# Projections between the blocks of two attentions, in a two-layer streaming encoder on one core

## The chip, the cores and the metric

One Trainium2 chip (trn2), one of its cores. The time is the device time of one execution in microseconds (us). Five engines work side by side, each on its own list of instructions: TensorE (matrix products and transposes, results in PSUM), VectorE, ScalarE, GpSimd, and SyncE, which here only issues DMA transfers. In the profile they are PE (PEld for its loads of the stationary operand), DVE, ACT, POOL and SP; a q behind the name is the part of an engine that issues DMAs.

## The reference

Two groups of tokens, 1024 of a prompt and 32 of a sample, pass through two post-norm layers with the same weights. Cut to what matters here, a layer is

```
(cq, kva, gq, gk, gv, gz, ga, gb, fq, fk, fv, ff) = split_cols(x @ w_in, IN_SPLITS)
o_a = attention(q_a, k_a, v_a, chunk_causal)                # latent: from low-rank cq and kva
o_b, s_new, conv_new = gated_deltanet(gq, gk, gv, gz, ...)  # 4 heads of 128
o_c = attention(fq, fk_all, fv_all, frame_causal, fcum)     # forgetting: fcum, running sum of log forgets
mix = jnp.concatenate([o_a, o_b, o_c], -1) @ w_out
x = layer_norm(ALPHA * x + mix, ...)
x = layer_norm(ALPHA * x + memory_attention(x, mem_k, mem_v, w_xq, w_xo), ...)
x = layer_norm(ALPHA * x + jnp.square(jax.nn.relu(x @ w_ff1)) @ w_ff2, ...)
```

with `mem_k = mem_prompt @ w_mk` and `mem_v = mem_prompt @ w_mv`, which depend on no activation. Both attentions have four heads with values of 64 features and sweep the 1024 queries in eight blocks of 128; block b reads the keys up to its own end, 128 (b + 1) of them. All is float32, and the caches, keys, values and states are outputs too.

## The kernel before, in words

Activations lie feature-major: features on the partitions, the 1024 + 32 tokens along the free axis, cut in three chunks of 352. Each operand of a large product is split in a rounded high part and the rest, and three products (high x high, high x low, low x high) add up in PSUM: `mm3`, lines 99 to 101. A projection's step (`proj`) is one chunk of one tile of 128 output features, 8 x 3 = 24 such products. Its weights come as a unit (`unit`): two DMAs on SP of 256 KB into two staging buffers (`ws`), a rounding on ScalarE (line 94) and a difference on VectorE (95), into two of eight buffers `w`. Other things share these eight: values, cached keys, unsplit weights.

A layer (`layer`) emits its work in this order: projections of delta-rule head 0 and a small tile `misc`; the memory's keys and values (`mem_kv`, 128 records on lines 1254 and 1267); the gates (from `misc`, first instruction line 249); delta-rule heads 0 to 3, each with serial chains and projections of the next head beside them; the sample's part of the delta rule; the low-rank projections (`mla_lora`); the forgetting attention's queries, keys and values (`fox_proj`, 12 steps of queries and keys, 9 of values) woven with keys and values of the cached latent rows (`mla_past`, 6 steps); the latent attention; the forgetting attention; the output projection of the mix, and the rest of the layer. Queries, keys and values of both attentions go to DRAM and are read back (`mla_head`, `fox_head`, `load_v`), one buffer `u` (six of 17 KB a partition) for a head.

Order: SP's DMA list is in the order written. On the other engines a planner at build time orders the instructions: of those that its model holds ready it takes the one emitted first. So what is emitted later fills gaps, if its operands and buffers are there.

Attention (`attend`, 744; pairs of heads `hp`, blocks `b`): for both heads the scores of a block are put in PSUM, in one piece up to 512 keys and in two beyond (banks `"wwwto"`: three of w, one of t, two of o), their maxima taken (758), a scale formed (760, 761), and the exponentials taken with their sums (767). The product with the values (`attend_out`, 786) of a block is put off until after the first exponentials of the next one (`later`): ScalarE copies the weights that TensorE turned by tiles of 128 keys (797, 799), TensorE multiplies them with the values (802), and the result goes to the mix in DRAM by POOL's queue. PSUM has eight banks: w 3, s 2, t 1, o 2.

Of the kernel before, what the change touches and what calls it, by code (L numbers as in the profile page):

```python
# [23 lines left out]
ALU = mybir.AluOpType  # L24
# [24 lines left out]
def weave(a, b, n):  # L49
    """Runs the generators a and b to their ends, n steps of b to each of a."""  # L50
    for _ in a:
        for _ in range(n):
            next(b, None)
    for _ in b:
        pass


class Net:
    def __init__(self, ctx, tc, I, O):
        self.tc, self.nc, self.I, self.O = tc, tc.nc, I, O  # L60
        self.sb = ctx.enter_context(tc.tile_pool(name="sb", bufs=1))
        self.pp = ctx.enter_context(tc.tile_pool(name="pp", bufs=1, space=bass.MemoryType.PSUM))
        self.dp = ctx.enter_context(tc.tile_pool(name="dp", bufs=1, space=bass.MemoryType.DRAM))
        self.n = 0
        self.last_pv = []
        self.nsc = self.nmx = 0
        self.todo = None

# [16 lines left out]

    def const(self, shape, dt, name):
        return self.sb.tile(shape, dt, tag=name, bufs=1, name=name)
# [15 lines left out]
    def unit(self, src, cols=1024, tags="ww"):  # L103
        """A piece of weights [128, cols], split."""
# [49 lines left out]
    def layer_norm(self, Y, g, b, X, c, dst, pe="", n=4):  # L154
        """pe: which of the sums, s of the features and q of the squares, TensorE takes over from VectorE."""
# [51 lines left out]
    def new_y(self, src, fill=True):  # L207
        """Y tiles, filled with the residual, or to be."""
# [12 lines left out]
    def proj(self, W, rhs, nk, evict, chunks=range(NCH), order=None):  # L221
        """W: (hi, lo) [128, nk, 128]; rhs(k, c) -> (hi, lo); evict(c, psum)."""
        for c in chunks:
            ps = self.ps("w")
# [18 lines left out]
    def gates(self, l, misc):  # L243
# [21 lines left out]
        # log(1 + e) = log(u) + (e - (u - 1)) / u, u = fl(1 + e)  # L265
# [6 lines left out]
        # beta = exp(min(x, 0)) / (1 + exp(-|x|))  # L272
# [8 lines left out]
        # g = -exp(a_log) * softplus(x)  # L281
# [7 lines left out]
        # running sums within a chunk, and the chunks' totals on every partition  # L289
# [16 lines left out]
        # rows of G, to be read back on every partition  # L306
# [79 lines left out]
    def gdn_norms(self, ssk, beta):  # L386
        """From the keys' sums of squares: 1 / rk, -beta rk^2, rk = 1 / norm."""
# [9 lines left out]
    def gdn_rq(self, q):  # L397
        """1 / norm of the queries, and the scale: sums on 32 partitions per group, four groups at once, then turned."""
# [64 lines left out]
    def gdn_inverse(self, Nt, beta):  # L463
        """T^T [128, chunk, 128] in the place of k.k: blocks of 16 by substitution, then doubled; the columns of gdn_norms."""
# [14 lines left out]
        # the diagonal, not decayed, holds the squares of the keys  # L479
# [5 lines left out]
        # blocks of 16 by substitution; through DRAM, a block (t, a) becomes a partition, twice over  # L485
# [14 lines left out]
        # 16 -> 32  # L500
# [8 lines left out]
        # 32 -> 64  # L509
# [4 lines left out]
        # the first products take places of T64 that hold nothing, or nothing any more  # L514
# [11 lines left out]
        # 64 -> 128  # L526
# [11 lines left out]
    def token_major(self, out, src, cols, n, scale):  # L538
        """[128 features, tokens] -> out [tokens, chunk, 128] scaled by a column per chunk."""
# [11 lines left out]
    def gdn_step(self, S, kT, qT, TT, Pt, kd, vs, eG, eGL, nb2, o, n, first=False):  # L551
        """One chunk of n tokens; the state S [dk, dv] -> the next; o [n, 128] receives the output."""
# [28 lines left out]
    def gdn_out(self, l, h, o, rq, z):  # L581
        """Normalise o [128, chunk, 128] by token, back to feature-major, gate, split, store to the mix."""
# [20 lines left out]
    def mix_tile(self, tag, m):  # L603
        """[128, hi | lo, m] and its second half, where the float32 values are put first."""
# [32 lines left out]
    def gdn_sample(self, l, gt):  # L637
        """The 32 sample tokens, one chunk, of the four heads."""
# [105 lines left out]
    def attend(self, heads, V, scale, tl, c0):  # L744
        """heads: for both the pieces (nk, width, fn) of their scores, fn(ps) emitting width of them, of which nk count.
        V: [128 keys, (head, 64)] by tile.  The weights are divided by their sum after the product with V."""
# [5 lines left out]
        pss = {}  # L752
        for h, pieces in enumerate(heads):
            for i, (nk, w, fn) in enumerate(pieces):
                self.nsc += 1
                ps = pss[h, i] = self.ps("wwwto"[self.nsc % 5])
                fn(ps[:, :w])
                nc.vector.reduce_max(mx[:, i, h:h + 1], ps[:, :nk], axis=AX.X)
        if n > 1:
            nc.vector.tensor_max(mx[:, 0], mx[:, 0], mx[:, 1])  # L760
        nc.vector.tensor_scalar_mul(nm, mx[:, 0], -scale)
        Ps = []
        for h, pieces in enumerate(heads):
            P = self.tl("r", [128, ROW], name="P")
            k0 = 0
            for i, (nk, w, fn) in enumerate(pieces):
                nc.scalar.activation(P[:, k0:k0 + nk], pss[h, i][:, :nk], AF.Exp, bias=nm[:, h:h + 1], scale=scale,
# [6 lines left out]
        # 64 times over, a column for each feature of the head  # L774
# [608 lines left out]
    def layer(self, l, X, xd, last):  # L1383
# [8 lines left out]
        for _ in self.mem_kv(l, M):  # L1392
            pass
# [271 lines left out]
```

## Time and profile before

| | |
|---|---|
| three runs | 3499.74, 3514.98 and 3519.27 us, median 3514.98 |
| profiled execution: span from its first to its last instruction | 3512.2 us |
| profiled execution: its own time | not given apart from the span |
| instructions | 57934 |
| mean granted clock of TensorE | 0.982 of full speed |
| DMA | 317.41 MB, mean 90 GB/s |

In rows of the profile, "x" is the count of instructions; busy time is the union of the instructions' times, the mean is in ns; "idle before" is the time the engine stood still before them, and behind the arrow stands what ended most of it. PEclk is the share of full clock that TensorE was granted. A busy share of TensorE near 100% does not mean that its products follow each other as closely as they can: their ends are modelled and overlap.

### The profile page before, as it was taken

Reading aid. Unit: us, or ns where it says so; the run is one execution under the profiler, and the core shown is the slowest. Engines: PE = TensorE matmul, PEld = TensorE weight load, DVE = VectorE, ACT = ScalarE, POOL = GpSimd, SP = SyncE. Lnnn points to the kernel's source line nnn. Section 1 sums busy time; section 2 is a strip of 40 time slices with the busy share of each in tenths; the row PEclk is TensorE's granted clock in tenths of the full one; section 3 lists DMA queues with packets and bytes.
Section 4 is the critical chain, followed back from the end, with each engine's and each line's share of the span. In section 5 each row is a group of like instructions: output and inputs, shape, how many; then the busy total and the mean of one; then the engine's idle time right before and its main releaser. Section 6 shows DMA issues by size and latency. Waiting matters only on the chain.

```text
span 3512.2 us, 57934 instructions
## 1 busy us (share of the span) xinstructions
PE 3393.6 (97%) x23108; PEld 3164.9 (90%) x23108; DVE 1800.0 (51%) x3936; ACT 1419.1 (40%) x3337; POOL 253.7 (7%) x418
## 2 busy tenths in 40 slices
PE   8989999999999999999999999999999999999998
PEld 7988879689899999999998887886898999999997
DVE  5667742556673333333655677335557633333336
ACT  5555544654452222222454554356535422222223
POOL 0101122100000000000010111221000000000000
PEclk9999999999999999999998999998999999999999
DMA  4423346553211111111142332464622111111111
GB/s 160 134 54 112 96 147 196 138 184 122 84 49 43 49 45 46 49 43 49 62 142 64 105 90 82 154 199 110 205 86 84 55 43 49 45 46 49 43 49 56
DMA packets 188182, 317.41 MB, mean 90 GB/s; under 512 B 46272, under 2 KB 98152, under 8 KB 187656
## 3 DMA queue, kind: packets, MB, share of 16 engines
q1 hardware_dynamic: 120176, 214.06, 19.7%
q0 software_dynamic: 30048, 90.75, 7.5%
q10 hardware_dynamic: 37688, 8.90, 1.4%
q8 instruction: 182, 2.98, 0.4%
q14 instruction: 88, 0.72, 0.1%
HBM read 224.99 MB, written 88.63 MB: 89 GB/s over the span
## 4 chain that ended last, share of the span: by engine, by line
PE 74%; issue 6%; DVE 5%; DMA 2%; ACT 2%; POOL 1%; ACTq 0%; DVEq 0%; POOLq 0%
PE psw L99 20%; PE psw L101 20%; PE psw L100 20%; PE pso L802 2%; PE pss L797 2%; PE pso L160 1%; PE pso L1306 1%; DVE Y L191 1%; PE psw L954 1%; PE psw L969 0%; DMA Gb<-gd 0%; PE pso L805 0%; PE psw L1210 0%; PE psw L1254 0%; PE psw L1267 0%
## 5 line engine op out<-in xcount | busy, mean ns | idle before, releaser
L99 PE MATMUL psw<-X,wu 128*128 128x352 f32 x2592 | 865.0, 334 | 8.9 <-ACT wu L94 3.5
L101 PE MATMUL psw<-X,wu 128*128 128x352 f32 x2592 | 857.4, 331 | 2.0 <-DVE wu L95 2.0
L100 PE MATMUL psw<-X,wu 128*128 128x352 f32 x2592 | 851.6, 329 | 2.6 <-DVE X L95 2.6
L94 ACT CAST wu<-ws 128x512 fp32r<-128x512 f32 x432 | 260.6, 618 | 802.2 <-PE psw L100 702.9
L99 PEld LDWEIGHTS psw<-X,wu 128*128 128x128 f32 x2592 | 495.0, 191 | 18.1 <-ACT wu L94 4.5
L100 PEld LDWEIGHTS psw<-X,wu 128*128 128x128 f32 x2592 | 495.4, 191 | 6.4 <-DVE X L95 2.9
L101 PEld LDWEIGHTS psw<-X,wu 128*128 128x128 f32 x2592 | 496.0, 191 | 5.7 <-DVE wu L95 3.3
L99 PE MATMUL psw<-hid,wu 128*128 128x352 f32 x1536 | 497.9, 324 | 1.9 <-DVE Y L1227 1.9
L101 PE MATMUL psw<-hid,wu 128*128 128x352 f32 x1536 | 498.3, 324 | 0.0
L100 PE MATMUL psw<-hid,wu 128*128 128x352 f32 x1536 | 498.1, 324 | 0.0
L95 DVE TENSOR_TENSOR wu<-ws,wu 128x512 fp32r<-128x512 f32 x432 | 291.3, 688 | 259.7 <-ACT wu L94 228.5
L1227 DVE TENSOR_TENSOR Y<-psw,Y 128x352 f32<-128x352 f32 x336 | 175.8, 524 | 351.7 <-PE psw L101 348.3
L99 PE MATMUL psw<-mo,wu 128*128 128x352 f32 x960 | 313.8, 327 | 5.2 <-DVE Y L1225 3.6
L100 PE MATMUL psw<-mo,wu 128*128 128x352 f32 x960 | 313.3, 326 | 0.0
L101 PE MATMUL psw<-mo,wu 128*128 128x352 f32 x960 | 313.2, 326 | 0.0
L99 PEld LDWEIGHTS psw<-hid,wu 128*128 128x128 f32 x1536 | 289.2, 188 | 2.7 <-DVE Y L1227 2.1
L101 PEld LDWEIGHTS psw<-hid,wu 128*128 128x128 f32 x1536 | 289.3, 188 | 0.6
L100 PEld LDWEIGHTS psw<-hid,wu 128*128 128x128 f32 x1536 | 289.4, 188 | 0.5
L1361 DVE TENSOR_TENSOR relu<-psw,relu 128x352 f32<-128x352 f32 x192 | 100.1, 522 | 247.8 <-ACT relu L1360 247.8
L1360 ACT ACTIVATE relu<-psw 128x352 f32<-128x352 f32 x192 | 88.5, 462 | 260.5 <-PE psw L101 258.4
L99 PEld LDWEIGHTS psw<-mo,wu 128*128 128x128 f32 x960 | 181.6, 189 | 7.5 <-DVE Y L1225 4.2
L101 PEld LDWEIGHTS psw<-mo,wu 128*128 128x128 f32 x960 | 182.2, 190 | 0.6
(498 smaller groups left out, 5101.8 us busy)
## 6 DMA issues: line engine op xcount, KB each, us to landing
ws<-in_w_ff_dram SPq DMA_DIRECT2D x256, 256.0 KB, 3.0
ws<-in_w_in_dram SPq DMA_DIRECT2D x100, 256.0 KB, 3.5
xd<-Y POOLq DMA_DIRECT2D x24, 704.0 KB, 3.9
X<-mix SPq DMA_DIRECT2D x96, 176.0 KB, 4.2
Y<-xd SPq DMA_DIRECT2D x24, 704.0 KB, 6.2
foxd<-fb POOLq DMA_DIRECT2D x24, 352.0 KB, 3.5
mix<-mxs POOLq DMA_DIRECT2D x32, 256.0 KB, 3.1
mix<-mxs POOLq DMA_DIRECT2D x64, 128.0 KB, 3.1
```

Of the source, the lines that this page charges most:

```text
L94: self.nc.scalar.copy(hi, src)
L95: (eng or self.nc.vector).tensor_sub(lo, src, hi.bitcast(F32))
L99: mm(ps, lhs[0], rhs[0], start=first, stop=False)
L100: mm(ps, lhs[0], rhs[1], start=False, stop=False)
L101: return mm(ps, lhs[1], rhs[0], start=False, stop=last)
L160: total = lambda ps, x, k=0, n=1: nc.tensor.matmul(ps[:, :CW], self.o1024, x, start=k == 0, stop=k == n - 1)
L191: nc.vector.tensor_mul(Yk, Yk, wide(rs))
L797: nc.tensor.transpose(pt[:, c:c + 128], Ps[h][:, 128 * k:128 * k + 128], self.ident)
L802: nc.tensor.matmul(po[64 * h:64 * h + 64, 0:128], V[k][:, 64 * h:64 * h + 64], PT[:, k - k0, h], start=k == 0, stop=k == kts - 1)
L1227: nc.vector.tensor_add(y, ps, y)
L1360: nc.scalar.activation(r, ps, AF.Relu)
L1361: nc.vector.tensor_mul(r, ps, r)
```

## The change

The memory's keys and values and most of the later projections are emitted between blocks of the attentions.

- `fill(n, *gens)` runs generators step by step; each `send(k)` emits steps until a share k / 72 of n steps is reached (72 = 2 `SCORED`, the key tiles of two pairs of heads); from k = 72 on all the rest.
- The latent attention has `fill` of the 21 steps of `fox_proj` and then the 6 of `mla_past`: five steps ahead of it, the others after its blocks, as many as the block has key tiles. `fox_proj` asks for the weights of its next tile one tile ahead.
- The forgetting attention has `fill` of `mem_kv`, now 8 steps (each half of the values by itself), whose tokens (1 MB) now lie in a buffer `u` and are loaded there.
- The blocks go 3, 4, 2, 5, 1, 6, 0, 7 in both attentions.
- `attend` does a head's scores, maxima, scale and exponentials before the next head's scores, with scores in the three banks w alone; projections that run as fill take t and o in turn (`psw`).
- Latent heads are loaded in pairs, the second pair after the first pair's blocks. The first two forgetting heads are loaded two blocks before the latent attention ends. The sample's latent attention moves into the forgetting attention, its own one to after the sixth block.

Comments are removed throughout; they are left out here. In `proj`, `mla_past`, `fox_proj` and `mem_kv`, `self.ps("w")` becomes `self.psw()`.

```diff
+SCORED = NT * (NT + 1) // 2
+BLOCKS = (3, 4, 2, 5, 1, 6, 0, 7)
+BLOCKS = [(b, sum(a + 1 for a in BLOCKS[:i + 1])) for i, b in enumerate(BLOCKS)]
...
+    def psw(self):
+        self.npw += 1
+        return self.ps(self.pw[self.npw % len(self.pw)])
...
+    def fill(self, n, *gens):
+        def run():
+            done = 0
+            k = yield
+            for g in gens:
+                for _ in g:
+                    done += 1
+                    while done * 2 * SCORED >= n * k and k < 2 * SCORED:
+                        k = yield
+            while True:
+                yield
+        g = run()
+        next(g)
+        return g
...
     def attend(self, heads, V, scale, tl, c0):
...
-        pss = {}
+        Ps = []
         for h, pieces in enumerate(heads):
+            pss = []
             for i, (nk, w, fn) in enumerate(pieces):
-                self.nsc += 1
-                ps = pss[h, i] = self.ps("wwwto"[self.nsc % 5])
+                ps = self.ps("w")
                 fn(ps[:, :w])
                 nc.vector.reduce_max(mx[:, i, h:h + 1], ps[:, :nk], axis=AX.X)
-        if n > 1:
-            nc.vector.tensor_max(mx[:, 0], mx[:, 0], mx[:, 1])
-        nc.vector.tensor_scalar_mul(nm, mx[:, 0], -scale)
-        Ps = []
-        for h, pieces in enumerate(heads):
+                pss.append(ps)
+            m = mx[:, :, h:h + 1]
+            if n > 1:
+                nc.vector.tensor_scalar(nm[:, h:h + 1], m[:, 0], m[:, 1], -scale, ALU.max, ALU.mult)
+            else:
+                nc.vector.tensor_scalar_mul(nm[:, h:h + 1], m[:, 0], -scale)
...
     def fox_proj(self, l, X):
...
+        W = self.k3(self.unit(I["w_in"][l, 16]), 8)
         for i in range(4):
-            W = self.k3(self.unit(I["w_in"][l, 16 + i]), 8)
+            Wn = self.k3(self.unit(I["w_in"][l, 17 + i]), 8) if i < 3 else [self.unit(I["w_fv"][l, i]) for i in range(2)]
...
+            W, us = Wn, Wn
-        us = [self.unit(I["w_fv"][l, i]) for i in range(2)]
...
-    def mem_kv(self, l, M):
+    def mem_kv(self, l):
...
+        M = self.tl("u", [128, 8, 256], name="ms")
+        nc.sync.dma_start(M, I["memT"])
...
     def layer(self, l, X, xd, last):
...
-        M = self.mem_load()
...
-        for _ in self.mem_kv(l, M):
-            pass
...
-        weave(self.fox_proj(l, X), self.mla_past(l), 1)
+        self.pw = "to"
+        fill = self.fill(21 + 6, self.fox_proj(l, X), self.mla_past(l))
+        fill.send(12)
+        step = self.gdn_sample_step(l, gt, TT, Gb)
         Vm = self.load_v(self.mvd)
-        A = [self.mla_head(h) for h in range(H)]
-        ms = self.mla_sample(l)
-        step = self.gdn_sample_step(l, gt, TT, Gb)
         for hp in range(2):
-            rest = ()
-            for b in range(NT):
+            A = [self.mla_head(2 * hp + i) for i in range(2)]
+            for i, (b, done) in enumerate(BLOCKS):
                 self.mla_attend(hp, A, Vm, b)
-                if hp == 1 and b == 1:
-                    rest = ms()
-                elif rest:
-                    rest[0]()
-                    rest = rest[1:]
-                if hp and b > 1:
+                fill.send(12 + hp * SCORED + done)
+                if hp and i > 1:
                     next(step, None)
+                if hp and i == 5:
+                    Af = [self.fox_head(h) for h in range(2)]
...
         Vf = self.load_v(self.fvd)
-        A = [self.fox_head(h) for h in range(H)]
-        fs = self.fox_sample(l)
-        rest = ()
+        ms = self.mla_sample(l)
+        A = Af + [self.fox_head(h) for h in range(2, H)]
+        fill = self.fill(8, self.mem_kv(l))
+        rest = ms()
         for hp in range(2):
-            for b in range(NT):
-                self.fox_attend(hp, A, Vf, b)
-                if hp == 0 and b == 3:
+            for i, (b, done) in enumerate(BLOCKS):
+                self.fox_attend(hp, A[2 * hp:2 * hp + 2], Vf, b)
+                fill.send(hp * SCORED + done)
+                if hp == 0 and i == 5:
+                    fs = self.fox_sample(l)
                     rest = fs()
...
         self.later(None)
+        self.pw = "w"
```

## Rows read from the trace of the kernel before

**Rows 1.** The page's busy times: us, share of the span, instructions.

```profile
PE 3393.6 (97%) x23108; PEld 3164.9 (90%) x23108; DVE 1800.0 (51%) x3936; ACT 1419.1 (40%) x3337; POOL 253.7 (7%) x418
```

**Rows 2.** Busy time by stretch, stages of both layers.

```profile
core 0: us, PE busy (x) PEld busy (x) DVE busy (x) ACT busy (x) POOL busy (x), PEclk, DMA share, GB/s
127.80:505.60 377.80, 354.82 (x3054) 313.82 (x3054) 256.26 (x711) 193.27 (x479) 57.66 (x97) 0.98 0.31 92
505.60:584.50 78.90, 78.90 (x529) 76.33 (x529) 12.58 (x22) 20.55 (x45) 26.41 (x46) 1.00 0.61 208
584.50:668.00 83.50, 82.35 (x698) 62.48 (x696) 48.72 (x159) 60.90 (x204) 11.19 (x17) 1.00 0.64 159
668.00:752.50 84.50, 79.42 (x698) 58.31 (x694) 43.38 (x144) 66.54 (x210) 11.44 (x17) 0.96 0.46 137
2238.20:2317.20 79.00, 79.00 (x530) 76.45 (x530) 12.57 (x22) 20.55 (x45) 26.32 (x46) 1.00 0.60 206
2317.20:2399.00 81.80, 80.25 (x654) 60.21 (x653) 46.26 (x153) 58.06 (x194) 10.54 (x16) 0.98 0.58 151
2399.00:2501.50 102.50, 92.06 (x765) 68.83 (x764) 48.54 (x157) 72.77 (x222) 12.81 (x19) 0.92 0.44 128
```

**Rows 3.** TensorE in order of time, layer 0: start, us, line, tiles.

```profile
99.97 13.97 PE L1254 MATMUL psw<-ms,wr 128*128 128x256 f32 x64
113.78 13.98 PE L1267 MATMUL psw<-wr,ms 128*128 128x256 f32 x64
127.69 0.58 PE L249 MATMUL pst<-cst,misc 32*128 32x32 f32 x7
```

**Rows 4.** The chain that ended last, start of layer 1: start, us.

```profile
1817.52 13.82 PE psw L1254 x64
1831.34 13.81 PE psw L1267 x64
```

**Rows 5.** VectorE in order of time, last silu of head 0.

```profile
104.11 1.26 DVE L240 TENSOR_TENSOR qkvz<-qkvz,sg 128x1056 f32<-128x1056 f32 x1 [3.50 <-ACT sg L239]
```

**Rows 6.** TensorE in order of time, end of the forgetting attention.

```profile
737.86 0.44 PE L797 MATMUL pss<-cst,P 128*128 128x128 f32 x2
...
741.79 1.04 PE L797 MATMUL pss<-cst,P 128*128 128x128 f32 x8
...
743.09 1.12 PE L802 MATMUL pso<-PT,V 128*64 128x128 f32 x16
...
745.03 0.32 PE L99 MATMUL psw<-X,wu 128*128 128x352 f32 x1
...
745.19 0.33 PE L100 MATMUL psw<-X,wu 128*128 128x352 f32 x1
...
748.35 0.66 PE L802 MATMUL pso<-PT,V 128*64 128x128 f32 x8
```

**Rows 7.** The latent heads' tiles: their loads.

```profile
DMA to landing us min/median/max: 14.5/14.9/17.0
```

**Rows 8.** Groups by line, 584.5 to 752.5: count, busy, mean ns, idle.

```profile
L767 ACT ACTIVATE P<-psw,sm 128x512 f32<-128x512 f32 (+5 forms) x58 | 34.3, 596 | 4.9 <-DMA mix<-mxs 2.5 <-DVE sm L761 1.3 <-issue 0.9
L767 ACT ACTIVATION_READ_ACCUMULATOR P<-psw,sm 128x1 f32 x58 | 12.4, 213 | 0.0
L758 DVE TENSOR_REDUCE sm<-psw 128x1 f32<-128x512 f32 (+5 forms) x58 | 32.1, 558 | 46.0 <-PE psw L814 37.9 <-PE psw L101 6.1 <-PE psw L1211 1.3
L761 DVE TENSOR_SCALAR sm<-sm 128x2 f32<-128x2 f32 x32 | 6.0, 188 | 0.7
```

**Rows 9.** SP's issues in order of time, before the output projection.

```profile
686.11 42.26 SPq L108 DMA_DIRECT2D ws<-in_w_out_dram  x8
...
728.42 8.15 SPq L1446 DMA_DIRECT2D X<-mix  x16
```

**Rows 10.** The forgetting heads' tiles: what ended TensorE's idle time.

```profile
  ACT P L767: 9.7, 16
```

More of the change, by code (lines that the diff above doesn't have):

```diff
@@ L46 @@
 C_ID, C_U, C_MG, C_EY1, C_FXS, C_HB, C_N = 0, 128, 256, 384, 416, 448, 450
[L49 to L54, printed above, removed]
-        pass
 class Net:
@@ L65, in __init__ @@
         self.last_pv = []
-        self.nsc = self.nmx = 0
+        self.nmx = self.npw = 0
+        self.pw = "w"
         self.todo = None
@@ L223, in proj @@
         for c in chunks:
-            ps = self.ps("w")
+            ps = self.psw()
             order = order or range(nk)
@@ L766, in attend @@
             for i, (nk, w, fn) in enumerate(pieces):
-                nc.scalar.activation(P[:, k0:k0 + nk], pss[h, i][:, :nk], AF.Exp, bias=nm[:, h:h + 1], scale=scale,
+                nc.scalar.activation(P[:, k0:k0 + nk], pss[i][:, :nk], AF.Exp, bias=nm[:, h:h + 1], scale=scale,
                                      accum_out=sm[:, i, h:h + 1])
@@ L981, in mla_past @@
         for hp in range(2):
-            ps = self.ps("w")
+            ps = self.psw()
             for k in range(2):
@@ L989, in mla_past @@
         for t in range(4):
-            ps = self.ps("w")
+            ps = self.psw()
             for k in range(2):
@@ L1077, in attend_pair @@
         cut = (0, ke) if ke <= 512 else (0, ke // 2, ke)
-        heads = [[scores(a, 128 * b, lo, hi) for lo, hi in zip(cut, cut[1:])] for a in A[2 * hp:2 * hp + 2]]
+        heads = [[scores(a, 128 * b, lo, hi) for lo, hi in zip(cut, cut[1:])] for a in A]
         self.attend(heads, [V[t // 4][:, t % 4, 128 * hp:128 * hp + 128] for t in range(NT)], scale, tl, 128 * b)
@@ L1111, in fox_proj @@
             c0 = 128 * t
-            ps = self.ps("w")
+            ps = self.psw()
             for k in range(8):
@@ L1236, in pair_units @@
         return U
-    def mem_load(self):
-        M = [self.tl("r", [128, 4, 256], name="ms") for _ in range(2)]
-        for i in range(2):
-            self.nc.sync.dma_start(M[i], self.I["memT"][:, 4 * i:4 * i + 4])
-        return M
-    def mem_kv(self, l, M):
+    def mem_kv(self, l):
         nc, I, O = self.nc, self.I, self.O
         self.kvd[l] = self.dp.tile([128, H, 768], F32, name=f"kvd_{l}", tag=f"kvd_{l}", bufs=1)
-        mt = lambda k: M[k // 4][:, k % 4]
+        M = self.tl("u", [128, 8, 256], name="ms")
+        nc.sync.dma_start(M, I["memT"])
         for h in range(H):
             W = self.raw_unit(I["w_mk"][l, h]).rearrange("p (k m) -> p k m", k=8)
-            ps = self.ps("w")
+            ps = self.psw()
             for k in range(8):
-                nc.tensor.matmul(ps[:, :256], W[:, k], mt(k), start=k == 0, stop=k == 7)
+                nc.tensor.matmul(ps[:, :256], W[:, k], M[:, k], start=k == 0, stop=k == 7)
             f = self.tl("q", [128, 256], name="mk")
@@ L1263, in mem_kv @@
             W = [self.raw_unit(I["w_mv"][l, i, j]).rearrange("p (k m) -> p k m", k=4) for j in range(2)]
-            ps = self.ps("w").rearrange("p (t n) -> p t n", t=2)
             for t in range(2):
+                ps = self.psw()
                 for k in range(8):
-                    nc.tensor.matmul(ps[:, t], mt(k)[:, 128 * t:128 * t + 128], W[k // 4][:, k % 4], start=k == 0, stop=k == 7)
-            f = self.tl("q", [128, 2, 256], name="mv")
-            nc.scalar.copy(f, ps)
-            nc.gpsimd.dma_start(O["mem_v"][l, :, 256 * i:256 * i + 256].rearrange("(t p) n -> p t n", p=128), f)
-            for t in range(2):
+                    nc.tensor.matmul(ps[:, :256], M[:, k, 128 * t:128 * t + 128], W[k // 4][:, k % 4], start=k == 0, stop=k == 7)
+                f = self.tl("q", [128, 256], name="mv")
+                nc.scalar.copy(f, ps[:, :256])
+                nc.gpsimd.dma_start(O["mem_v"][l, 128 * t:128 * t + 128, 256 * i:256 * i + 256], f)
                 nc.gpsimd.dma_start(self.kvd[l][:, 2 * i:2 * i + 2, 512 + 128 * t:640 + 128 * t],
-                                    f[:, t].rearrange("p (h n) -> p h n", h=2))
-            yield
+                                    f.rearrange("p (h n) -> p h n", h=2))
+                yield
     def mem_scores(self, q, KV, c):
@@ L1391, in layer @@
         y = self.gdn_proj(l, 0, X, [(W, lambda c, ps: nc.scalar.copy(misc[:, c * CW:(c + 1) * CW], ps))])
-        for _ in self.mem_kv(l, M):
-            pass
         gt = self.gates(l, misc)
@@ L1435, in layer @@
         self.later(None)
+        self.pw = "w"
         M = self.new_x()
```

## The prediction

> **What bounds the kernel now.** Read the page's busy times first [rows 1]: TensorE is busy 97% of the span, so nothing off it can be worth much by itself. But a busy TensorE is not one at its peak, and the second view, busy time by stretch [rows 2], shows where it isn't. In the projections before the latent attention of layer 0 (505.6 to 584.5) weight loads fill 76.33 of 78.9 us. In the latent attention (584.5 to 668) they fill 62.48 of 83.5, in the forgetting one (668 to 752.5) 58.31 of 84.5, and there ScalarE, which takes every exponential and copies every turned block of weights, is busy 66.54. The third view gives prices from dense places [rows 6]: projection products of 352 columns start 0.16 us apart (745.03, 745.19), so 0.455 ns a column; two turned blocks take 0.44 us and eight 1.04, so 0.10 for one more; eight products with the values take 0.66 and sixteen 1.12, so 0.0575 for one more.
>
> With these a layer's two attentions can be added up. The code gives 36 key tiles for a pair of heads, so 4 x 72 = 288 turned blocks (28.8 us) and twice as many records with the values (33.1). A head's scores add to 4736 columns over its eight blocks (no piece under 256), three products each in the latent, two in the forgetting attention: 4736 x 4 x 5 x 0.455 ns = 43.1. Masks and reciprocals, 96 at some 0.07 (estimate), 7; the sample's attentions and the sample's delta step, estimated at the same prices, 13; the output projection's first products, which fill the end already, some 2.4. Demand is 127.5 us: latent 69.4, forgetting 58.1. The stretches are 168.0 us in layer 0 and 184.3 in layer 1 [rows 2], so 40.5 and 56.8 us are open, 97 together. Of that some 13 us is clock: the granted clock is 0.96 in the forgetting stretch of layer 0 and 0.98 and 0.92 in the two of layer 1, each a mixture of the two levels, 1.2 and 2.4 GHz (share below 1 times length: 3.4, 1.6, 8.2).
>
> The Trainium skill, "Perfetto Trace Analysis", section "Identifying the Most-Contended Engine", says that matmul busy time misjudges the headroom of TensorE and that the share of weight loads is to be read instead. By busy time only 1.15 + 5.08 + 1.55 + 10.44 = 18 us would be open in the four stretches, and no more than 18 could be won; by the weight loads' reading, which the sum above bears out, it is 97. I go by the sum.
>
> **The change, part by part.** (1) The memory's keys and values leave the start of a layer. There TensorE does nothing else for 99.97 to 127.76, 27.8 us, and the gates' first transpose follows at 127.69 [rows 3]; in layer 1 the same two lines stand in the chain that ended last, 13.82 + 13.81 [rows 4]. What follows was ready but for the gates: the last silu of head 0 ends at 105.4 [rows 5]. The loss of cover is small, since the next head's projections (4 x 3 x 24 products at 0.16, 46 us) need only weights. The chain moves up by at least 127.7 - 105.4 = 22 us and at most by 27.8; I take 26 a layer, as this view shows nothing else between.
>
> (2) These 27.8 us of products come back in the forgetting attention. Open there: 84.5 - 58.1 = 26.4 in layer 0, 44.4 in layer 1. (3) Of the 21 steps of later projections and 6 of cached rows, five run ahead of the latent attention; the other 22 go between its blocks. All of the 78.9 us of that stretch [rows 2] still have to be done; latent attention with them is 69.4 + 78.9 - 4 (the sample's attention moves to the forgetting stretch) = 144.3 us of TensorE.
>
> How well will TensorE fill? Below: 127.8 to 505.6, where projections lie beside the delta rule's serial chains, has weight loads for 313.82 of 377.8, against 76.33 of 78.9 in pure projections: 0.83 / 0.97 = 0.86. Above: 0.99, pure projections. In the latent stretch over half of the work waits for nothing but weights, and ScalarE has 60.90 + 20.55 = 81 us to do in some 150: I take 0.94, 153.5 us. In the forgetting stretch fill is 27.8 of 58.1 - 2.4 + 4 + 27.8 = 87.5, and ScalarE's 66.54 with the sample's and the fill's copies is near 75. Bounds: 0.99 gives 88.4; fill that falls into no gap gives 84.5 + 27.8 + 4 = 116. I take 0.88, in between, 99.4 us.
>
> (4) New waits at the seams. Only two latent heads are held at a time, so heads 2 and 3 are loaded after the last scores of 0 and 1; such a load lands 14.9 us after its issue [rows 7]. Beside it lie three fill steps (3 x 24 x 256 columns, 8.4 us) and the last block's product with the values (16 x 0.10 + 32 x 0.0575 = 3.4): 3 us open, from nothing up to 15. At the start five steps (5 x 24 x 0.16, 19 us) lie beside the store of the last keys and the first two heads' load: 0 to 15, I take 2. At the end weights of the output projection now queue on SP behind the memory's, whose buffers they need; before, SP issued them over 686 to 728 and the mix from 728 [rows 9]. What was filled at the tail (2.4 us) goes and some us of load show: 3, up to 15. Sum 8 a layer, ends 0 and 45.
>
> (5) Scores lose two of five PSUM banks, and each head's exponentials follow its own scores. VectorE takes a scale for each head, 64 a layer in place of 48 scales and maxima of 0.19 us [rows 8], 3 us beside 48.72 busy of 83.5: nothing. A block of two pieces a head has four pieces for three banks; the fourth waits for maximum, scale and first exponential: 0.558 + 0.188 + 0.596 + 0.213 = 1.56 us [rows 8]. There are 32 such blocks, 50 us, all of it beside a fill step or the block before's products, from both of which TensorE can draw: I take nothing, the other end is 50. (6) Stores on POOL (11 us busy in the latent stretch, 26 more come) and the 16 memory stores instead of 14 lie beside; nothing, at most their wait for ScalarE's copies, which is in 0.94. Blocks in the order 3, 4, 2, 5, 1, 6, 0, 7 cost nothing themselves; they put a light block beside a heavy one. (7) Whether fewer gaps keep the clock up is inside the two shares; it is at most the 13 us.
>
> **The sum.** Layer 0 before: 27.8 + 78.9 + 83.5 + 84.5 = 274.7. Layer 1: 27.8 + 79.0 + 81.8 + 102.5 = 291.1. After, each: 153.5 + 99.4 + 8 = 260.9, and 1.8 of the first part's 27.8 not regained: 262.7. Gain 12.0 + 28.4 = 40 us. The profiled execution's span is 3512.2; its whole time isn't given apart, and the median of the three runs, 3514.98 (3499.74 to 3519.27), lies 2.8 above the span, so I take the sum from there: 3515 - 40 = 3475.
>
> **Rivals.** *Full fill* (0.17): everything open is filled at 0.99 and the seams are covered: 145.8 + 88.4 = 234.2 a layer, 97 us won less 4: 3422. For it: the sources of fill are independent of the attention. Against: no stretch with exponentials comes near, 0.86 is the best beside chains.
>
> *The gaps move* (0.20): the bank wait of part 5 stays uncovered in the larger part of its 50 us, since the order of TensorE's instructions is set when the program is built, or ScalarE's exponentials queue behind evictions. 40 won, 38 to 50 given back: 3513 to 3525, and I name 3517. For it: what TensorE waits for longest before products of the forgetting heads is the exponentials, 9.7 us in 16 waits [rows 10], with five banks. The Trainium skill, "Perfetto Trace Analysis", section "Optimization Strategy", reads gaps that repeat as a sign of too little PSUM for the next tile, which speaks against taking banks away; no run here yet shows three.
>
> *The seams open* (0.13), the slower side: loads now stand where nothing hides them. Both loads of latent heads lie open whole (15 + 15) and the output projection's weights 15: 45 a layer in place of 8, 74 us more: 3475 + 74 = 3549. It decides from 8 + 20 = 28 us a layer on. For it: SP issues in the order written, the mix behind 42 us of weights that wait for buffers [rows 9], so one waiting load holds up all fill weights behind it; the second pair's load can't be early, its buffers are the first pair's. Against: fill steps stand on either side of each seam.
>
> That the change doesn't do what it says would be fill that is issued in a lump before or after the blocks; it is the second rival with the same price.
>
> **How the numbers follow.** Forecast 0.50: 3475 with its own range 3450 to 3497. About 0.5% (17.6 us) is what a measurement here tells from no change. Faster: the forecast and full fill, 0.67. Same: the gaps move, 0.20. Slower: the seams, 0.13. The range for 8 in 10 runs from 3430, which leaves out some half of full fill, to 3526, which leaves out most of the slower cases.
>
> **What would show it.** Right: no memory products near 100 and 1817, the gates there some 26 us earlier; weight loads of at least 0.88 of the latent stretch and 0.80 of the forgetting one; granted clock near 1.00 in both; two layers' stretches of some 261 each. Wrong: weight-load share unchanged and the stretches longer by the moved work; TensorE's waits on the exponentials grown from a few us to tens (banks); or gaps of 10 us or more ended by a DMA at the change of heads, at the first scores, or before the output projection (seams). If the start of a layer shrinks by far less than 22 us, part 1 was wrong: another chain was as late.

## The result, and the profile after

The changed kernel is slower: 3531.47 us (median of 4 runs, 3523.15 to 3537.18) against 3511.82 for the kernel before beside it (4 runs, 3499.74 to 3519.27), a ratio of 1.0064, interval 1.0043 to 1.0084. The forecast was 3475, so the sum is wrong by some 60 us and has the wrong sign; the time lies above the range too. The page's busy times of the changed kernel, which answer to [rows 1]:

```profile
PE 3396.5 (96%) x23108; PEld 3154.2 (90%) x23108; DVE 1804.5 (51%) x3968; ACT 1424.7 (40%) x3341; POOL 256.6 (7%) x422
```

They hardly differ from before. The busy time by stretch, which answers to [rows 2], does: by core, the length of a stretch, busy time of each engine, granted clock, DMA share and GB/s. The edges are the gates' first transpose (100.6), the last step of the latent keys and values (478.0, in layer 1 2219.2), the first latent scores (496.5, 2237.6), the first forgetting scores (642.1, 2380.7) and the last product with the values (774.8, 2506.2).

```profile
100.60:478.00 377.40, 358.39 (x3031) 319.24 (x3031) 261.60 (x715) 203.45 (x493) 55.62 (x94) 0.97 0.33 96
478.00:496.50 18.50, 18.50 (x147) 16.52 (x146) 4.03 (x12) 2.85 (x8) 4.25 (x7) 1.00 0.96 245
496.50:642.10 145.60, 138.76 (x1051) 113.96 (x1049) 53.83 (x168) 77.08 (x237) 34.45 (x57) 0.99 0.51 149
642.10:774.80 132.70, 121.49 (x870) 89.59 (x867) 53.04 (x169) 75.02 (x222) 20.32 (x32) 0.89 0.50 151
2219.20:2237.60 18.40, 18.40 (x140) 16.37 (x139) 4.46 (x13) 3.10 (x9) 4.04 (x7) 1.00 0.88 242
2237.60:2380.70 143.10, 138.36 (x1051) 113.89 (x1049) 54.10 (x168) 77.21 (x237) 34.35 (x57) 0.99 0.53 157
2380.70:2506.20 125.50, 117.91 (x879) 87.50 (x877) 52.37 (x169) 74.29 (x223) 20.34 (x32) 0.95 0.50 153
```

The latent part with its fill takes 18.5 + 145.6 = 164.1 and 161.5 us, forecast 153.5 + 5 = 158.5. The forgetting part takes 132.7 and 125.5, forecast 99.4 + 3 = 102.4: that is where the sum broke. Weight loads fill only 89.59 of 132.7 there (0.68; I asked for 0.80, and an unchanged share, 0.69 before by [rows 2], was a sign of being wrong) and 0.80 of the latent part (I asked for 0.88).

The start of a layer did move up. The timeline of TensorE, against [rows 3]:

```profile
100.55 0.71 PE L251 MATMUL pst<-cst,misc 32*128 32x32 f32 x9
```

That is 27.1 us ahead of the seven transposes of [rows 3] (the other two of the nine had run at 53.4); the first running sum of the forget gates, some steps on, is 20.9 earlier (136.1 before, 115.2 after).

One more pair of views bears on why little was filled: what TensorE's weight loads waited for, in the two attentions of layer 0, before (584 to 752) and after (496 to 775). Columns: total us, times, longest us; "issue" is a wait for nothing that the profile shows.

```profile
PEld pso L802 <- ACT PT L799: 10.4, 32, 0.9
PEld L814 <- issue: 7.5, 35, 0.3
PEld pso L805 <- issue: 5.3, 31, 0.2
PEld pss L797 <- issue: 4.2, 24, 0.2
```

```profile
PEld pso L821 <- ACT PT L818: 11.1, 33, 1.0
PEld L833 <- issue: 8.5, 33, 0.5
PEld psw L1231 <- ACT P L786: 7.5, 7, 1.5
PEld pss L816 <- ACT P L786: 5.8, 5, 1.9
PEld pso L824 <- issue: 5.5, 32, 0.2
PEld psw L844 <- ACT P L786: 5.0, 2, 3.6
PEld pss L816 <- issue: 4.5, 24, 0.3
```

The reader is to see that the waits before products with the values (for the copy of the turned blocks), masks, reciprocals and transposes are nearly the same in both: 27.4 us before, 29.6 after, some 120 waits of 0.1 to 1 us. I had counted them as open. The fill went around them, and waits for exponentials (P) came on top, 12.5 us of them by scores that need a bank (L1231 of the forgetting heads, L844 of the sample).

### The profile page after: what moved, and what is told of

Same layout as the page of the kernel before. It is cut to its first block, busy times and chain, and to the rows that moved or that the text cites. A ratio compares the mean times of both kernels' runs of the same rounds, so it can differ in the third digit from the quotient of the medians.

```text
span 3521.4 us, 57972 instructions
## 1 busy us (share of the span) xinstructions
PE 3396.5 (96%) x23108; PEld 3154.2 (90%) x23108; DVE 1804.5 (51%) x3968; ACT 1424.7 (40%) x3341; POOL 256.6 (7%) x422
## 4 chain that ended last, share of the span: by engine, by line
PE 78%; issue 7%; DVE 7%; DMA 4%; ACT 3%; POOL 1%; ACTq 0%; SPq 0%; DVEq 0%; POOLq 0%
PE psw L102 19%; PE psw L101 19%; PE psw L103 19%; PE pso L821 2%; PE pss L816 2%; PE pso L162 1%; DMA mix<-mxs 1%; PE pst L101 1%; DVE Y L193 1%; PE pso L1321 1%; PE pst L102 1%; PE pst L103 1%; PE psw L1231 1%; DMA Gb<-gd 1%; PE pso L102 1%
## 5 line engine op out<-in xcount | busy, mean ns | idle before, releaser
L101 PE MATMUL psw<-X,wu 128*128 128x352 f32 x2400 | 793.6, 331 | 5.6 <-ACT X L96 3.0
L102 PE MATMUL psw<-X,wu 128*128 128x352 f32 x2400 | 793.4, 331 | 2.4 <-DVE X L97 1.8
L103 PE MATMUL psw<-X,wu 128*128 128x352 f32 x2400 | 792.4, 331 | 2.7 <-DVE wu L97 2.5
L101 PE MATMUL psw<-hid,wu 128*128 128x352 f32 x1536 | 496.5, 323 | 1.8 <-DVE Y L1248 1.8
L101 PEld LDWEIGHTS psw<-X,wu 128*128 128x128 f32 x2400 | 458.2, 191 | 11.4 <-ACT X L96 3.5
L103 PEld LDWEIGHTS psw<-X,wu 128*128 128x128 f32 x2400 | 458.2, 191 | 6.7 <-DVE wu L97 4.6
L102 PEld LDWEIGHTS psw<-X,wu 128*128 128x128 f32 x2400 | 457.6, 191 | 6.5 <-DVE X L97 2.2
```

The source lines that it names most:

```text
L101: mm(ps, lhs[0], rhs[0], start=first, stop=False)
L102: mm(ps, lhs[0], rhs[1], start=False, stop=False)
L103: return mm(ps, lhs[1], rhs[0], start=False, stop=last)
```

## The experiments

Each kernel was timed in five rounds beside the kernel before. Ratios are to that; the stages (layer 0 / layer 1, us) are read from each one's timeline of TensorE. "Start" is the first running sum of the gates in layer 0, "latent" goes from the last key and value step to the first forgetting score (projections ahead of the attention included), "forgetting" from there to the last product with the values.

| kernel | ratio to before | interval | start | latent | forgetting |
|---|---|---|---|---|---|
| before | 1 | | 136.1 | 159.5 / 161.2 | 87.6 / 97.4 |
| changed | 1.0064 | 1.0043 to 1.0084 | 115.2 | 164.1 / 161.5 | 132.7 / 125.5 |
| mem_start | 1.0071 | 1.0048 to 1.0093 | 137.0 | 162.7 / 160.1 | 110.1 / 108.7 |
| mem_only | 1.0135 | 1.0106 to 1.0164 | 116.5 | 159.8 / 165.8 | 131.9 / 135.1 |
| five_banks | 1.0067 | 1.0047 to 1.0088 | 112.7 | 160.1 / 159.2 | 128.3 / 133.9 |
| lane | 1.0064 | 1.0046 to 1.0082 | 115.5 | 164.8 / 161.9 | 131.9 / 124.7 |
| order | 1.0101 | 1.0080 to 1.0122 | 136.4 | 170.5 / 171.7 | 98.8 / 99.9 |
| attend3 | 1.0028 | 1.0014 to 1.0042 | 138.2 | 168.1 / 163.5 | 93.9 / 95.5 |
| natural | 1.0012 | 0.9992 to 1.0031 | 116.5 | 161.9 / 161.1 | 123.6 / 118.9 |
| sample_later | 1.0080 | 1.0059 to 1.0101 | 115.4 | 159.1 / 158.4 | 138.2 / 124.4 |
| mem_eighth | 0.9909 | 0.9886 to 0.9932 | 116.8 | 163.4 / 161.7 | 104.7 / 100.6 |
| lump | 1.0108 | 1.0082 to 1.0134 | 116.3 | 173.4 / 176.1 | 125.4 / 122.5 |
| natural5 | 1.0073 | 1.0049 to 1.0098 | 116.1 | 164.0 / 162.4 | 129.9 / 132.4 |
| start5 | 1.0064 | 1.0041 to 1.0088 | 136.7 | 172.8 / 172.3 | 95.6 / 95.9 |
| two_heads | 1.0089 | 1.0067 to 1.0112 | 137.5 | 173.3 / 171.9 | 88.8 / 96.9 |
| mem_split | 1.0118 | 1.0093 to 1.0142 | 117.9 | 166.8 / 166.8 | 127.3 / 126.7 |
| mem_delta | 1.0062 | 1.0041 to 1.0083 | 110.9 | 159.4 / 159.6 | 88.8 / 97.3 |

### First set: which part of the change

**mem_start**, memory back at the start:

```
+        for _ in self.mem_kv(l, M):      # ahead of the gates, M loaded as before
+            pass
-        fill = self.fill(8, self.mem_kv(l))
+        fill = self.fill(8, iter(()))
```

> The changed kernel with the memory's keys and values back at the start of a layer; the latent fill, three banks and block order stay. Three theories. (A) In the forgetting attention the memory's products are added, not filled in: they cost there the 27.8 us a layer that they cost at the start, and this kernel takes what the changed one takes, 3523 to 3540 us. (B) Moving them was a gain by itself (the start shrinks by 26 us a layer, the forgetting attention grows by less), and the loss lies in the latent part: slower than the changed kernel by 20 to 50 us. (C) In the forgetting attention they cost more than at the start, through late loads and a lower clock: faster than the changed kernel by 10 to 30 us, with a forgetting stretch of some 90 us and a clock near 1.00 in it.

3534.08 us, theory A: no difference. The start is 21.8 us later and the forgetting part 22.6 and 16.8 shorter. And that part without any fill is still far longer than before:

```profile
664.50:774.60 110.10, 100.17 (x753) 71.73 (x752) 50.19 (x165) 68.53 (x210) 10.77 (x16) 0.84 0.40 112
2406.80:2515.50 108.70, 97.91 (x752) 69.78 (x752) 50.38 (x165) 68.20 (x210) 10.77 (x16) 0.86 0.38 108
```

110.1 against 87.6 (108.7 against 97.4), with the clock at 0.84 and 0.86 (before 0.96 and 0.92 [rows 2]), so some of the loss isn't the memory's at all.

**mem_only**, the kernel before with the memory moved:

```
                 self.fox_attend(hp, A, Vf, b)
+                if b % 2:
+                    next(mem, None)
```

> The kernel before with the memory's keys and values alone moved, a step after every second block of the forgetting attention; five banks, blocks in order and the projections ahead of the latent attention as before. (A) added, not filled in: as the kernel before, 3503 to 3520 us. (B) a gain by itself: 3470 to 3495. (C) costs more than at the start: 3525 or more.

3562.74 us, theory C, 50 above the kernel before: the forgetting part grows by 44.3 and 37.7 for 27.8 us of products.

**five_banks** and **lane**, the two waits that I could name:

```
-                ps = self.ps("w")                # scores
+                ps = self.psw()
-        self.pw = "to"
+        self.pw = "wwwto"
```

```
-            nc.scalar.dma_start(self.mix[2 + h, :, :, SEQ:T], ...)
+            nc.gpsimd.dma_start(self.mix[2 + h, :, :, SEQ:T], ...)
```

> The changed kernel with scores and fill taking their banks in turn from all five (three, one, and one of the outputs' two) in place of three for scores and the others for the fill. If the three banks cost the time (waits of TensorE on the exponentials of the forgetting heads, 5 to 8 us a layer in the profile, and more behind them): faster than the changed kernel by 10 to 40 us. If not: within 6 us of it.

> The changed kernel with the four stores of the delta rule's sample step issued on POOL in place of ScalarE. In the changed kernel SP's queue stands for 19.3 us (18.8 in layer 1) at a load of the past's positional keys behind a store of the mix, and the forgetting heads 2 and 3 and the memory behind it. If that wait costs the time (the first sample scores 2.7 us late, no fill until 666 us, the clock at 0.75 over 640 to 680): SP's wait is gone and the kernel is faster by 8 to 25 us. If the loads are early enough anyway: within 5 us.

3534.95 and 3534.41 us: neither decides. With five banks the scores' waits for exponentials do go, in layer 0 from 7.5 and 5.0 us to 1.5 and 1.3, but the transposes' waits for them grow from 5.8 to 8.0, and a memory step, which now shares the banks, waits 5.0. Five banks for the scores alone were not tried on the changed kernel. In SP's timeline of the changed kernel the wait is plain:

```profile
618.42 20.96 SPq L1073 DMA_DIRECT2D mlaK<-in_kpe_past_dram  x2
653.75 0.37 SPq L1265 DMA_DIRECT2D ms<-in_memT_dram  x1
```

With the stores on POOL it is gone (1.06 us for these two at 623.02), but SP then stands 12.2 us at the next load (in two waits), for stores of cached values. The memory's load is issued 1 us ahead of the first forgetting scores (650.68 and 651.8) where it was 12 us behind them (653.75 and 642.1), and still the first memory product starts 22.7 us after these scores in place of 24.5 (674.48, 666.57). The wait was real and decided nothing. Nor does a load hold that product back in `lane`: the DMA share is 0.05 over 664.3 to 670, and the product follows the scores ahead of it without a wait. It comes where TensorE's list has it.

### Second set: order, softmax, seam

**order** and **attend3** put one part each on the kernel before; **natural** and **sample_later** take one back from the changed kernel:

```
-            for b in range(NT):                               # order
+            for i, b in enumerate((3, 4, 2, 5, 1, 6, 0, 7)):
```

```
-BLOCKS = (3, 4, 2, 5, 1, 6, 0, 7)                             # natural
+BLOCKS = (0, 1, 2, 3, 4, 5, 6, 7)
```

```
-        rest = ms()                                           # sample_later
+        rest = ()
+                if hp == 0 and i == 1:
+                    rest = ms()
```

attend3 is the changed `attend` in the kernel before, nothing else.

> The kernel before with its blocks in the order 3, 4, 2, 5, 1, 6, 0, 7 alone. With the memory back at the start the changed kernel still takes 36 us more in its two layers' attentions than the kernel before (272.7 and 268.8 us from the last key and value step to the last product with the values, against 247.0 and 258.6). If the order of the blocks makes it (heavy blocks at the change of attentions): slower than the kernel before by 15 to 40 us. If not: within 8 us.

> The kernel before with the changed softmax alone: scores from three banks, the exponentials of a head right behind its own scores. If the banks or that order make the 36 us: slower than the kernel before by 15 to 50 us. If the wait is covered, or if five banks on the changed kernel told all: within 8 us.

> The changed kernel with its blocks in order 0 to 7. If the new order costs time: faster than the changed kernel by 10 to 30 us. If it is of use, as a light block beside a heavy one: slower by 5 to 20. If the order is no matter: within 5 us.

> The changed kernel with the latent sample's attention emitted after the second block of the forgetting attention in place of ahead of the first. If its scores at the seam hold TensorE up (4 us idle before them, then the clock at 0.76 for 40 us): faster than the changed kernel by 8 to 25 us. If the seam is short of work whatever comes first: within 5 us.

3544.22, 3519.18, 3518.75 and 3536.71 us. The order alone costs the kernel before 1.0%, 35 us, some 18 a layer in the attentions, and taken back it wins 13 us (18 by the ratios) from the changed kernel, which then ties with the kernel before. The stretches of `order`, latent attention and forgetting attention of each layer:

```profile
597.00:688.30 91.30, 86.87 (x690) 64.47 (x689) 46.54 (x153) 59.55 (x198) 10.61 (x16) 0.93 0.57 142
688.30:787.10 98.80, 89.75 (x716) 65.88 (x714) 47.19 (x152) 69.72 (x214) 12.14 (x18) 0.90 0.38 112
2348.40:2440.80 92.40, 86.12 (x685) 63.48 (x684) 45.79 (x151) 60.37 (x197) 10.62 (x16) 0.94 0.54 134
2440.80:2540.70 99.90, 89.88 (x705) 64.73 (x703) 47.47 (x153) 69.90 (x215) 12.14 (x18) 0.88 0.38 111
```

The work is that of before [rows 2], the stretches are longer and the clock is lower, 0.93, 0.90, 0.94 and 0.88: by share below 1 times length 34 us, where it was 13, so some 20 of the 35 us show as a lower clock. A block's product with the values is put off into the next block's softmax; in rising order each covers one a tile larger, in this order block 0 stands before block 7 and covers next to nothing. That this is the mechanism is argued from the code, not shown. The softmax alone costs 10 us in the kernel before. The sample's place at the seam is no matter (1.0080 against 1.0064, well inside the intervals).

### Third set: how much is filled

All in order 0 to 7. **mem_eighth** leaves out seven of eight memory products. **lump** emits all latent fill ahead of the first block (`fill.send(2 * SCORED)` in place of 12). **natural5** has the scores of both heads first and five banks; **start5** is the same with the memory at the start.

```
-            for k in range(8):                                # mem_eighth
-                nc.tensor.matmul(ps[:, :256], W[:, k], M[:, k], start=k == 0, stop=k == 7)
+            nc.tensor.matmul(ps[:, :256], W[:, 0], M[:, 0], start=True, stop=True)
```

> The changed kernel with blocks in order 0 to 7 (3518.75 us), and of the memory's products one in eight left, with the same loads, evictions and stores: 24.2 us a layer of TensorE less, its output is not the reference's. If the products are added to the forgetting attention, not filled into it: 48 us faster, 3465 to 3476. If they lie in open time: within 10 us of 3518.75. In between, the share filled is what is missing to 48.

> The changed kernel with blocks in order 0 to 7, and all 27 steps of later projections and cached rows emitted ahead of the latent attention's first block, none between its blocks. If fill between the blocks takes open time: slower than 3518.75 by 8 to 20 us. If the attention's open time is made of waits too short for a fill step (the copy of the turned blocks, masks, reciprocals: 30 us a layer in the kernel before and the same with fill): within 6 us of it.

> The changed kernel with blocks in order 0 to 7 and the scores of both heads ahead of the exponentials over five banks, as before; the fill takes its banks from the same five. The changed softmax alone cost the kernel before 10 us: if it costs that here, 3503 to 3512; if fill covers it, within 5 us of 3518.75.

> The same with the memory's keys and values at the start of a layer: of the change only the fill of the latent attention, its two heads at a time and its sample's attention in the forgetting part are left. If that fill is a gain by itself: 3480 to 3500 us. If it is worth nothing: 3505 to 3520. If two heads at a time and the sample at the seam cost: above 3520.

mem_eighth: 3479.73 us, 39 less than `natural` (36 by the ratios), where 48 us of products are gone. So by these figures three quarters to four fifths of the memory's products are added to the forgetting part and one part in four or five lies in open time; the intervals of the two ratios leave some 11 us either way on the 36, so half of them to nearly all are added. The two forgetting stretches give 18.9 + 18.3 = 37 us. The forgetting stretches of `natural` and of `mem_eighth`:

```profile
653.20:776.80 123.60, 117.92 (x876) 88.70 (x873) 53.32 (x171) 73.52 (x223) 20.93 (x33) 0.93 0.52 154
2390.50:2509.40 118.90, 115.35 (x877) 87.65 (x875) 53.74 (x171) 73.80 (x223) 20.94 (x33) 0.94 0.52 154
```

```profile
652.10:756.80 104.70, 96.59 (x768) 68.61 (x766) 52.25 (x171) 71.35 (x223) 21.07 (x33) 0.92 0.59 182
2365.50:2466.10 100.60, 94.35 (x768) 67.53 (x766) 52.09 (x171) 71.33 (x223) 21.02 (x33) 0.93 0.63 195
```

lump: 3545.91 us, 27 above `natural` (34 by the ratios). Both my theories missed: fill between the blocks is worth more than I allowed for. Its stretches, projections and latent attention of each layer:

```profile
481.70:566.30 84.60, 79.81 (x556) 74.34 (x554) 11.77 (x26) 17.33 (x41) 26.33 (x46) 0.97 0.67 210
566.30:655.10 88.80, 82.62 (x648) 61.49 (x646) 45.95 (x154) 61.50 (x204) 11.31 (x18) 0.95 0.40 103
2225.80:2314.10 88.30, 80.22 (x547) 74.78 (x546) 12.13 (x27) 17.50 (x42) 26.24 (x46) 0.97 0.65 200
2314.10:2401.90 87.80, 81.70 (x643) 60.82 (x641) 45.86 (x154) 61.43 (x203) 11.28 (x17) 0.95 0.40 106
```

The latent attention is 88.8 and 87.8 us here, without the sample's attention, against 80.3 and 81.8 (to the first forgetting score) with it in the kernel before. So the change made this attention longer and its fill regained that: from the last key and value step to the first forgetting score it is 173.4 and 176.1 us here, 161.9 and 161.1 in `natural`. Fill did find room there, 11.5 and 15.0 us. natural5 (3538.86) missed both its ranges: the old softmax on banks shared with the fill is some 20 us slower than three banks of its own (1.0073 against 1.0012); whether by the sharing or by the order of the scores is not separated. start5 (3534.14) is above 3520, its third theory: the latent fill without the moved memory, on that softmax, is slower than the kernel before.

### Fourth set: what made the latent attention longer, and other places for the memory

```
+            if hp:                                            # two_heads
+                A = [self.mla_head(h, A[h - 2]) for h in (2, 3)]
```

```
         self.gdn_head(l, 0, gt, y)                            # mem_delta
+        M = self.mem_load()
+        for _ in self.mem_kv(l, M):
+            pass
```

`mem_split` is `mem_only` with the softmax of `attend3`, and its memory steps in banks t and o. In `mem_delta` the memory's tokens also move, into two of the eight buffers w, which the projections' weights need.

> The kernel before with the latent heads 2 and 3 loaded into the places of heads 0 and 1, so only after the last scores of these, and nothing else. If the load stands open at the change of heads (14.9 us from issue to landing, less the last block's product with the values of 3.4 us): slower than the kernel before by 15 to 25 us in both layers together. If the blocks' own work covers it: within 8 us.

> The kernel before with the memory moved to the forgetting attention, a step behind every second block, and with the changed softmax: scores from three banks, the memory's steps from the other two kinds, nothing shared between scores and fill. The memory moved alone with shared banks cost 50 us, the changed softmax alone 10. If the shared banks made the 50: 3510 to 3530 us. If the place made it (late loads, blocks in order without fill in the latent part): 3555 or more.

> The kernel before with the memory's keys and values emitted after the first head of the delta rule in place of ahead of the gates. The start shrinks by 21 us a layer as in the changed kernel; TensorE's open time in the delta rule is some 29 us a layer, as short waits. If the products find a fifth of their 28 us there, as in the forgetting attention: within 12 us of the kernel before, 3500 to 3512. If chains of the delta rule have longer gaps: 3470 to 3495. If they hold up the chain of head 1: slower, above 3520.

two_heads: 3542.83 us, 31 slower by the ratio, above the 15 to 25 of the first theory; the two latent parts hold 24.5 of it. Loading the latent heads two at a time, which the fill needs because the activations hold four of six buffers, costs 13.8 and 10.7 us a layer where nothing covers it. What its TensorE waited for in 585 to 680:

```profile
PE psw L99 <- DMA mlaA<-kped: 5.4, 1, 5.4
PE pso L802 <- ACT PT L799: 1.7, 4, 0.7
```

5.4 us are the wait itself; the clock is 0.91 over the stretch (1.00 before [rows 2]), some 8 us more. mem_split: 3546.46, between the two theories, and its interval overlaps mem_only's (1.0093 to 1.0142, 1.0106 to 1.0164): that shared banks are a part of mem_only's 50 us is not shown, and they are not all of it. mem_delta: 3533.96, slower: the start gains 25 us, but the stretch from the first running sum to the last key and value step is 411.3 us against 369.2 (411.2 against 384.3); the two buffers w may have a part in that. Three places for the memory's products were tried, and the one of the kernel before is the best.

## Why the prediction was wrong

**The step that failed** is the one that called 40.5 and 56.8 us a layer "open" and let part 2 put 27.8 us of memory products into the forgetting part at a share of 0.88. Open is not the same as free. By the waits above, some 27 us of the 40.5 in layer 0 are short waits within a block's own sequence, and they are there nearly unchanged with the fill beside them (they are waits of the weight loads; by busy time TensorE's products stand still for only 6.2 us of these stretches); the short prices from dense places left them out of the demand. That such waits take no fill is read from their being the same with it, not shown by a run of its own; and in the latent part fill did find room (lump). Measured, the memory's products found room for a quarter to a fifth of themselves (mem_eighth), where I let the forgetting stretch grow by 9.9 us a layer for them, the sample's attention and the seam (92.5 before on average, 102.4 forecast). It grew by 36.6, to 129.1; in order 0 to 7 by 28.7. A second cause stands beside the short waits: the fill comes late. No memory product lies in the first 24.5 us of the forgetting part of layer 0 (22.9 in layer 1, 19.7 and 17.4 in `natural`), where TensorE's granted clock is 0.71 (0.79 in layer 1). The changed kernel's stretches, the first forgetting scores being at 642.1 and the first memory product at 666.57:

```profile
640.00:660.00 20.00, 17.16 (x91) 10.43 (x92) 8.09 (x30) 9.59 (x31) 1.35 (x2) 0.76 0.97 224
660.00:680.00 20.00, 17.88 (x114) 14.02 (x115) 6.37 (x19) 7.50 (x23) 1.78 (x3) 0.75 0.49 170
```

With the loads earlier the fill was as late (lane); an earlier place for it in TensorE's list was not tried, so how the missing room divides between short waits and late fill is open.

**The order of the blocks**, which I priced at nothing in one sentence, costs 13 to 18 us in the changed kernel, 35 without fill (natural, order). I looked at how heavy and light blocks share the fill, not at which block covers which softmax.

**The softmax over three banks**, priced at nothing, costs the kernel before 10 us. On the changed kernel five shared banks give no gain (1.0067 against 1.0064) though the scores' waits for banks go, so *the gaps move* is not what made the loss, even if waits for exponentials did grow as that rival said. The Trainium skill, "Perfetto Trace Analysis", section "Optimization Strategy", which that rival cited for gaps as a sign of too little PSUM, is neither borne out nor refuted: the five banks were shared with the fill.

The Trainium skill, "Perfetto Trace Analysis", section "Identifying the Most-Contended Engine", judges TensorE's headroom by the share of its weight loads, and led me to read their free time as headroom: they are free for 29% of the four attention stretches (102 of 352 us), yet the memory's products were mostly added. In the forgetting part the share of busy time was nearer: it leaves 15.5 us in both layers before, and 11 to 12 us of the products found room. In the latent part it was not: lump's attention leaves 6.2 and 6.1 us by busy time, and the fill regained 11.5 and 15.0.

**The seams** (8 a layer) were not measured one by one in the changed kernel. Open, the change of latent heads alone is 11 to 14 us a layer (two_heads), and the latent part with its fill came out 5.6 and 3.0 us over the forecast, so there the fill covers most of it. The change of attentions, where the fill comes late, was in no term of the sum. *The seams open*, the slower rival, is then not shown either: the 19 us that SP stands are real, and taking them away wins nothing. The result is on that rival's side for another reason.

**The start** moved as said, 27 us at the gates' first instruction, 21 to 22 at the first running sum, where I took 26. The memory's records end in both ledgers: 21 saved, 20 paid.

**The sum by stages**, from the profiled executions (3512.2 and 3521.4, so 9 us apart where the runs are 20 apart). Forecast was too low by 30.3 and 23.1 us in the forgetting part, 5.6 and 3.0 in the latent part, 5 and 5 at the start: 72 us. Against that the delta-rule stretch, in which nothing was changed, was 6.4 and 20.4 us shorter; in layer 1 its granted clock was 0.93 before and 0.98 after, 27 against 7 us lost, which is nearly all of the 20. That stretch varied from 363 to 382 us in layer 0 between kernels with the same work there (mem_delta apart), which I can't explain beyond the clock; it is why I go by the ratios and not by one ledger. Another 5 us are no change at all: my stretch of layer 1 ran to 2501.5, past the last product with the values at 2496.4.

**The clock**, in part 7 at most 13 us to be won, went the other way: 0.89 and 0.95 in the forgetting part, 14.6 and 6.3 us lost, where before it was 3.4 and 8.2. The first memory step shows it, 16 records in 5.34 us at a granted clock of 0.67, where 27.8 / 8 = 3.5 is the usual:

```profile
666.57 5.34 PE L1270 MATMUL pst<-ms,wr 128*128 128x256 f32 x16
```

**Left open**: the mechanism of the order, how the missing room divides between short waits and late fill, the rest of mem_only's 50 us, and why mem_delta loses more than the products take. No version that does all the work beats the kernel before; `natural` ties with it (0.9992 to 1.0031).

## What to carry to other kernels

Before moving work into a stretch's idle time, list its waits by length: some 120 waits of 0.2 us on average stayed here as they were beside the fill, and a probe that drops most of the moved products tells in one run how much is hidden. Price what makes room for the fill (fewer buffers, another order, loads in halves) as if nothing covered it, for the fill pays that back first. In a pipeline where one block's tail covers the next block's head, ask what an order that sets a light block before a heavy one costs by itself: here 35 us.

## What the runs showed of the hardware

A load on SP stood behind stores issued by ScalarE for other data: 19.3 us at a load of an input, gone when those stores were issued by POOL (lane). Whether the chip or the program's own waits made it so is not shown. And a seam cost more than its wait: in two_heads 5.4 us of waiting at the change of heads came with some 8 us lost to a granted clock of 0.91 over the 94 us around it, a mixture of the chip's two levels, 1.2 and 2.4 GHz.
